# Main tiles of 128 positions of four batches, in five equal groups, in a load-heavy running-maximum kernel

## The chip, the cores and the metric

The kernel runs on one core of one Trainium2 chip. The metric is the device time of one execution in microseconds (us), median of several runs.

## The reference

```python
B, S, D = 8, 2048, 4096            # x is 268 MB of float32, w has 4096 elements
proj = (x @ w).squeeze(-1)         # one dot product per batch and position
cm = np.maximum.accumulate(proj, axis=1)
is_record = (proj >= cm).astype(np.float32)
return np.cumsum(is_record, axis=1)     # [8, 2048]
```

Every byte of `x` is used once. The scans afterwards are over 2048 values in each of 8 rows, so they are small.

## The kernel before

Positions 0 to 1919 are handled in four groups of 512, 512, 512 and 384 positions. A main tile is one batch of one group. Each of the 128 partitions gets `r` consecutive rows, `r` being 4 (a 64 KB run) or 3 (48 KB). Three buffers of 64 KB per partition take turns.

```python
for g in range(NG):                       # 4 groups, RS = (4, 4, 4, 3)
    r = RS[g]
    for t in range(B):                    # 8 tiles, one batch each
        i = SY.dma_start(
            out=at(g, t)[:, : r * D],
            in_=x[B - 1 - t, STARTS[g] : STARTS[g] + r * P, :].rearrange(
                "(p r) d -> p (r d)", r=r),
        ).then_inc(xs[t], 16)
        ...                               # waits until the tile three before is used up
```

Each row's dot product is divided by columns. VectorE multiplies and sums columns 0 to 2815 in one instruction. GpSimd multiplies columns 2816 to 4095 in place, and ScalarE then sums those products. At the end of a group, TensorE turns the partial sums into rows of 8 batches, and VectorE runs the scans.

```python
for j in range(r):
    i = dot(xb[:, j * D : j * D + VC], w_v[:, :VC], sum_v[...])      # VectorE
...
i = G.tensor_mul(out=xl, in0=xl, in1=w_sb).then_inc(pl, 1)           # GpSimd, one row
...
i = add_up(at(g, t)[:, j * D + VC : (j + 1) * D], sum_p[...])        # ScalarE
...
T.matmul(out=ps[:B, j : r * P : r], lhsT=l[...], rhs=identity, ...)  # 2 per row of the tile
```

The last 128 positions, the tail, come in tiles of 32 positions of four batches (2.1 MB, partitions ordered position first, then batch). The last two of these tiles are cut into smaller pieces. The change leaves this part alone, apart from the buffers it lands in.

## Time and profile before

| | before |
|---|---|
| time, median of 3 runs | 630.12 us |
| span in the profile | 629.3 us |
| busy: VectorE (DVE), GpSimd (POOL), ScalarE (ACT) | 65%, 59%, 29% |
| load queue, share of the 16 DMA engines' time | 98.9% |
| bytes read | 268.45 MB |

The first fence is from the page of the kernel before: busy time, the span in 40 slices (tenths busy), the load queue, and the chain of waits by engine.

```profile
PE 29.1 (5%) x96; PEld 13.5 (2%) x96; DVE 407.3 (65%) x294; ACT 181.2 (29%) x274; POOL 370.7 (59%) x149
...
DVE  0755775556766567755578655676556976655897
...
POOL 0554675456765557745577555676557666555775
...
DMA  9999999999999999999999999999999999999996
...
q1 hardware_dynamic: 6544, 268.50, 98.9%
...
DMA 16%; POOL 3%; DVE 2%; issue 1%; PE 1%; ACT 0%; SPq 0%
```

Only the DMA row has no gap. VectorE and GpSimd are five to seven tenths busy almost everywhere. The chain names only about a quarter of the span. It stops at 483 us, so its shares say little here.

The better reading comes from the moments at which loads land. GpSimd's first product of a tile waits for nothing but its load, so the timeline of GpSimd shows them. The columns are start, duration, line, operation and count, and in brackets the idle time just before and what ended it.

```profile
179.06 11.49 POOL L276 TENSOR_TENSOR xall<-xall,w_sb 128x1280 f32<-128x1280 f32 x4 [7.80 <-DMA xall<-in_x_dram]
198.36 11.50 POOL L276 TENSOR_TENSOR xall<-xall,w_sb 128x1280 f32<-128x1280 f32 x4 [7.81 <-DMA xall<-in_x_dram]
217.66 11.51 POOL L276 TENSOR_TENSOR xall<-xall,w_sb 128x1280 f32<-128x1280 f32 x4 [7.80 <-DMA xall<-in_x_dram]
...
512.45 8.64 POOL L276 TENSOR_TENSOR xall<-xall,w_sb 128x1280 f32<-128x1280 f32 x3 [5.86 <-DMA xall<-in_x_dram]
526.95 8.63 POOL L276 TENSOR_TENSOR xall<-xall,w_sb 128x1280 f32<-128x1280 f32 x3 [5.86 <-DMA xall<-in_x_dram]
...
609.34 2.90 POOL L336 TENSOR_TENSOR xall<-xall,w_sb 128x1280 f32<-128x1280 f32 x1 [0.39 <-DMA xall<-in_x_dram]
614.20 2.90 POOL L336 TENSOR_TENSOR xall<-xall,w_sb 128x1280 f32<-128x1280 f32 x1 [1.52 <-DMA xall<-in_x_dram]
```

Tiles of 8.39 MB come 19.30 us apart, tiles of 6.29 MB 14.50 us apart, and the tail's 2.10 MB tiles 4.86 us apart. These are 435, 434 and 432 GB/s. After each big tile GpSimd idles 7.8 us.

### The profile page before, as it was taken

The page shows a single profiled execution, that of the slowest core. Times are in us where ns is not written, and L with a number is a line of the kernel's source. Part 1 is how long each engine was busy: PE and PEld are TensorE (multiplying, and loading weights), DVE is VectorE, ACT ScalarE, POOL GpSimd, SP SyncE. Part 2 cuts the span into 40 slices and gives each one's busy share as a digit, 9 for nine tenths or more (in the row PEclk, how much of TensorE's full clock was granted, in tenths as well). Part 3 has the DMA queues.
Part 4 walks back from the last instruction along what each step waited for, and adds up shares of the span by engine and source line. Part 5 has one row for each costly group of instructions (what it writes and reads, how often), then busy time and mean ns, then how long its engine had stood idle before and what let it go on. Part 6 is the DMA issues. An engine that isn't in the chain of part 4 may idle for free. (4 is left out here: it accounts for less than half of the span.)

```text
span 629.3 us, 1140 instructions
## 1 busy us (share of the span) xinstructions
PE 29.1 (5%) x96; PEld 13.5 (2%) x96; DVE 407.3 (65%) x294; ACT 181.2 (29%) x274; POOL 370.7 (59%) x149
## 2 busy tenths in 40 slices
PE   8000000000020000000001000000002000000100
PEld 3000000000010000000000000000001000000000
DVE  0755775556766567755578655676556976655897
ACT  1222332223322233222233222332223232232254
POOL 0554675456765557745577555676557666555775
PEclk9999999999999999999996555555555555555565
DMA  9999999999999999999999999999999999999996
GB/s 401 400 467 400 446 421 425 442 437 429 442 425 450 417 450 417 459 408 458 408 458 408 458 408 458 408 459 408 462 418 438 416 447 441 413 447 444 404 425 248
DMA packets 6563, 268.54 MB, mean 427 GB/s; under 512 B 760, under 2 KB 1016, under 8 KB 1568
## 3 DMA queue, kind: packets, MB, share of 16 engines
q1 hardware_dynamic: 6544, 268.50, 98.9%
q10 hardware_dynamic: 16, 0.02, 0.0%
q14 instruction: 3, 0.02, 0.0%
HBM read 268.45 MB, written 0.07 MB: 427 GB/s over the span
## 5 line engine op out<-in xcount | busy, mean ns | idle before, releaser
L124 DVE CUSTOM_DVE_ANT_0 xall<-xall,w_v 128x2816 f32<-128x2816 f32 (+1 forms) x129 | 385.5, 3041 | 181.8 <-DMA xall<-in_x_dram 181.8
L276 POOL TENSOR_TENSOR xall<-xall,w_sb 128x1280 f32<-128x1280 f32 x120 | 345.0, 2909 | 246.7 <-DMA xall<-in_x_dram 243.3
L130 ACT ACTIVATE xall<-xall 128x1280 f32<-128x1280 f32 (+2 forms) x130 | 162.9, 1253 | 428.6 <-POOL xall L276 408.3
L312 PE MATMUL ps<-identity,small 128*8 128x128 f32 x60 | 13.0, 406 | 568.6 <-PEq L309 568.6
L130 ACT ACTIVATION_READ_ACCUMULATOR xall<-xall 128x1 f32 x130 | 24.2, 186 | 0.0
L336 POOL TENSOR_TENSOR xall<-xall,w_sb 128x1280 f32<-128x1280 f32 (+2 forms) x8 | 21.1, 2632 | 3.1 <-DMA xall<-in_x_dram 3.0
L312 PEld LDWEIGHTS ps<-identity,small 128*8 128x8 f32 x60 | 7.3, 125 | 575.4 <-issue 571.3
L140 DVE TENSOR_TENSOR_SCAN cm<-ps,cm,small 8x512 f32<-8x512 f32 (+3 forms) x8 | 7.0, 869 | 18.8 <-PE ps L312 18.4
L224 PE MATMUL w_v<-w,identity 8*128 8x512 f32 x14 | 12.1, 1056 | 0.0
L124 DVE DVE_READ_ACCUMULATOR2_ANT small<- 128x1 f32 x133 | 10.8, 81 | 0.0
L246 DVE MEMSET ps<- 8x512 f32 x1 | 0.5, 485 | 15.7 <-ACT w L235 15.7
L146 DVE TENSOR_TENSOR_SCAN cnt<-ps,cnt,small 8x512 f32<-8x512 f32 (+3 forms) x8 | 7.0, 870 | 0.3
L224 PEld LDWEIGHTS w_v<-w,identity 8*128 8x128 f32 x14 | 4.6, 332 | 7.3 <-issue 7.3
L143 DVE TENSOR_TENSOR ps<-ps,cm 8x512 f32<-8x512 f32 (+3 forms) x8 | 3.9, 487 | 0.3
L232 ACT COPY w_sb<-w_v 128x768 f32<-128x768 f32 x1 | 0.8, 799 | 11.4 <-PE w_v L224 11.4
L347 POOL TENSOR_TENSOR masked<-fold,small 128x4 f32<-128x4 f32 x8 | 1.6, 201 | 3.2 <-DVE small L124 3.2
L124 DVE CUSTOM_DVE_ANT_0 xall<-xall,w_v,small 128x480 f32<-128x480 f32 (+2 forms) x4 | 3.1, 810 | 0.2 <-DVE small L124 0.2
L357 PE MATMUL ps<-fold,masked 128*8 128x32 f32 x20 | 2.0, 235 | 25.3 <-ACT masked L352 17.7
L352 ACT ACTIVATE masked<-fold,small 128x4 f32<-128x4 f32 x10 | 3.0, 298 | 0.3
L336 POOL TENSOR_TENSOR xall<-xall,w 128x640 f32<-128x640 f32 (+1 forms) x2 | 2.3, 1137 | 0.1
L224 PE MATMUL ps<-w,identity 8*128 8x512 f32 x2 | 2.1, 1135 | 2.6 <-DMA w<-in_w_dram 2.6
L231 ACT ACT_TABLE_LOAD x1 | 1.3, 1283 | 2.7 <-DVE fold L242 2.7
(18 smaller groups left out, 5.3 us busy)
## 6 DMA issues: line engine op xcount, KB each, us to landing
xall<-in_x_dram SPq DMA_DIRECT2D x8, 6144.0 KB, 33.5
xall<-in_x_dram SPq DMA_DIRECT2D x6, 2048.0 KB, 42.4
xall<-in_x_dram SPq DMA_DIRECT2D x1, 1264.0 KB, 36.6
xall<-in_x_dram SPq DMA_DIRECT2D x1, 816.0 KB, 39.3
xall<-in_x_dram SPq DMA_DIRECT2D x1, 784.0 KB, 37.9
xall<-in_x_dram SPq DMA_DIRECT2D x2, 240.0 KB, 26.6
xall<-in_x_dram SPq DMA_DIRECT2D x1, 416.0 KB, 39.4
xall<-in_x_dram SPq DMA_DIRECT2D x24, 45.0
```

The source lines that it names most:

```text
L124: return V.tensor_tensor_reduce(out=xsl, in0=xsl, in1=wsl, scale=1.0, scalar=seed, op0=ALU.mult, op1=ALU.add, accum_out=dst,)
L130: return A.activation(out=xsl, in_=xsl, func=ACTF.Copy, accum_out=dst)
L140: V.tensor_tensor_scan(out=cm_, data0=src, data1=low, initial=cm0, op0=ALU.max, op1=ALU.max,)._wait_ge(psr, base).then_inc(psr, 1)
L143: V.tensor_tensor(out=src, in0=src, in1=cm_, op=ALU.is_ge)._wait_ge(psr, base + 1).then_inc(psr, 1)
L146: V.tensor_tensor_scan(out=cnt_, data0=src, data1=low, initial=cnt0, op0=ALU.add, op1=ALU.max,)._wait_ge(psr, base + 2).then_inc(cs, 1)
L224: i = T.matmul(out=dst, lhsT=identity[:NW, k : k + 1].to_broadcast([NW, P]), rhs=w_row, start=True, stop=True,).then_inc(bw, 1)
L276: i = G.tensor_mul(out=xl, in0=xl, in1=w_sb).then_inc(pl, 1)
L312: i = T.matmul(out=ps[:B, j : r * P : r], lhsT=l[:, j * B : (j + 1) * B], rhs=identity, start=k == 0, stop=k == 1,)
L336: G.tensor_mul(out=xl, in0=xl, in1=w_pool(*p))._wait_ge(xq[i], 16).then_inc(pl, 1)
L347: return eng.tensor_tensor(out=e, in0=by_b, in1=acc.to_broadcast([P, H]), op=ALU.mult)
L352: return A.activation(out=e, in_=by_b, func=ACTF.Copy, scale=acc)._wait_ge(pa, na).then_inc(ms, 1)
L357: return T.matmul(out=ps[:B, k * Q : (k + 1) * Q], lhsT=masked[:, n * B : (n + 1) * B], rhs=by_i, start=start, stop=stop,)
```

## The change

Its intent is one loop with equal tiles. The main part becomes five groups of 384 positions, each of six tiles. A tile holds 128 positions of four batches, and each partition still gets one 64 KB run (four consecutive rows of one batch). The differently sized last group disappears, and so does the code that existed only for it. GpSimd multiplies four rows in one instruction. Since a tile now mixes four batches over the partitions, GpSimd adds and masks the sums before TensorE turns them. The last main tile is loaded in two halves, so that work on it can start earlier. The diff, cut to its core:

```diff
-    RS = (4, 4, 4, 3)
-    R = RS[0]
+    R = 4
+    NC = 3
+    NT = NC * B // H          # 6 tiles a group
+    N = NC * P                # 384 positions a group
+    NG = 5
...
-            for t in range(B):
-                    in_=x[B - 1 - t, STARTS[g] : STARTS[g] + r * P, :].rearrange(
-                        "(p r) d -> p (r d)", r=r
+            for t in range(NT):
+                b0, s0 = t % 2 * H, STARTS[g] + t // 2 * P
+                src = x[b0 : b0 + H, s0 : s0 + P, :].rearrange(
+                    "b (q r) d -> q b (r d)", r=R
+                )
+                if last and g == NG - 1:          # two halves
+                    i = SY.dma_start(out=at(t)[:, :half], in_=src[:, :, :half]).then_inc(xs[t], 16)
+                    SY.dma_start(out=at(t)[:, half:], in_=src[:, :, half:]).then_inc(xh, 16)
+                else:
+                    i = SY.dma_start(out=at(t), in_=src).then_inc(xs[t], 16)
...
-                    i = G.tensor_mul(out=xl, in0=xl, in1=w_sb).then_inc(pl, 1)
+                n = R // 2 if t == NT - 1 else R
+                for j in range(0, R, n):
+                    xl = rows[:, j : j + n, VC:]
+                    i = G.tensor_mul(out=xl, in0=xl, in1=w_one.to_broadcast([P, n, PC])).then_inc(pl, 1)
+            G.tensor_tensor(out=sum_t, in0=sum_v, in1=sum_p, op=ALU.add)...
+            G.tensor_tensor(out=gmask..., in0=sum_t..., in1=by_b..., op=ALU.mult)...
...
-            for j in range(r):
-                for k, l in enumerate((sum_p, sum_v)):
-                        out=ps[:B, j : r * P : r], lhsT=l[:, j * B : (j + 1) * B],
-                        rhs=identity, start=k == 0, stop=k == 1,
+            for j in range(R):
+                for c in range(NC):
+                        out=ps[:B, c * P + j : (c + 1) * P : R],
+                        lhsT=gmask[:, k * B : (k + 1) * B],
+                        rhs=by_i, start=True, stop=True,
```

More of the change, by code (lines that the diff above doesn't have):

```diff
@@ L41 @@
     NW = D // WC
-    RS = (4, 4, 4, 3)
-    R = RS[0]
+    R = 4
     NS = 3
-    NG = len(RS)
-    NL = NG - 1
-    N = R * P
-    STARTS = [sum(RS[:g]) * P for g in range(NG)]
-    S0 = sum(RS) * P
-    assert S0 + P == S
+    H = 4
+    Q = P // H
+    NC = 3
+    NT = NC * B // H
+    N = NC * P
+    NG = 5
+    STARTS = [g * N for g in range(NG)]
+    S0 = NG * N
+    assert S0 + P == S and NT % NS == 0
     VC = 2816
@@ L53 @@
     CV = 3584
-    H = 4
-    Q = P // H
     LAST = [
@@ L87 @@
     w_sb = sb([P, PC], "w_sb")
-    cm = sb([B, N], "cm")
-    cnt = sb([B, N], "cnt")
+    cm = sb([B, N + P], "cm")
+    cnt = sb([B, N + P], "cnt")
+    gmask = sb([P, R * NC * B], "gmask")
     masked = sb([P, 10 * B], "masked")
@@ L102, in cut @@
         return small[:, off[0] - n : off[0]]
-    sum_v, sum_p = cut(R * B), cut(R * B)
+    sum_v, sum_p, sum_t = (cut(R * NT) for _ in range(3))
     acc_v, acc_p = cut(B - 2), cut(B - 2)
@@ L112, in sem @@
         return tc.alloc_semaphore(f"{name}_{next(ns)}")
-    xs = [sem("xs") for _ in range(B)]
-    fr = [sem("fr") for _ in range(B)]
+    xs = [sem("xs") for _ in range(NT)]
+    fr = [sem("fr") for _ in range(NT)]
     xq = [sem("xq") for _ in TILES]
-    ws, bw, wc, cs, od, oe, psr, pd, pl, go, sd, pa, con, fo, ms, p7, mg, pg, ml = (
-        sem(n) for n in "ws bw wc cs od oe psr pd pl go sd pa con fo ms p7 mg pg ml".split()
+    ws, bw, wc, cs, od, oe, psr, pd, pl, xh, sd, pa, con, fo, ms, p7, mg, pg, ml, mk = (
+        sem(n) for n in "ws bw wc cs od oe psr pd pl xh sd pa con fo ms p7 mg pg ml mk".split()
     )
@@ L148, in scans, with at, col_of @@
         )._wait_ge(psr, base + 2).then_inc(cs, 1)
-    def at(g, t):
-        return xbuf[(t if g < NL else t + NS - 1) % NS]
+    def at(t):
+        return xbuf[t % NS]
     def user_before(g, t):
-        if t >= NS:
-            return t - NS, g + 1
-        if g == NL:
-            return B - NS + t, g
-        return max(u for u in range(B) if u % NS == t), g
+        return (t - NS, g + 1) if t >= NS else (t + NT - NS, g)
     def free(u, n):
-        return (p7, n) if u == B - 1 else (fr[u], 2 * n)
+        return (p7, n) if u == NT - 1 else (fr[u], 2 * n)
+    def col_of(t, j):
+        return (j * NC + t // 2) * 2 + t % 2
     with tc.tile_critical(no_gpsimd_drain=True):
         for g in range(NG):
-            r = RS[g]
-            for t in range(B):
-                i = SY.dma_start(
-                    out=at(g, t)[:, : r * D],
-                    in_=x[B - 1 - t, STARTS[g] : STARTS[g] + r * P, :].rearrange(
-                        "(p r) d -> p (r d)", r=r
-                    ),
-                ).then_inc(xs[t], 16)
-                u, n = user_before(g, t)
+            for t in range(NT):
[3 more added lines that the diff above has]
+                )
+                half = R // 2 * D
+                last = t == NT - 1
+                u, n = user_before(g, t)
+                if last and g == NG - 1:
+                    i = SY.dma_start(
+                        out=at(t)[:, :half], in_=src[:, :, :half]
+                    ).then_inc(xs[t], 16)
+                    SY.dma_start(
+                        out=at(t)[:, half:], in_=src[:, :, half:]
+                    ).then_inc(xh, 16)
+                else:
+                    i = SY.dma_start(out=at(t), in_=src).then_inc(xs[t], 16)
+                    if last:
+                        SY.sem_inc(xh, 16)
                 if n:
-                    i._wait_ge(*(free(u, n)))
+                    i._wait_ge(*free(u, n))
                 if g == t == 0:
@@ L182 @@
                     SY.dma_start(
-                        out=out[:, STARTS[g - 1] : STARTS[g]], in_=cnt
+                        out=out[:, STARTS[g - 1] : STARTS[g]], in_=cnt[:, :N]
                     )._wait_ge(cs, g + 1).then_inc(od, 16)
         def slot(m):
-            if m < NS:
-                return None, xbuf[m][:, RS[-1] * D :]
-            u = B - NS if m < 2 * NS else B - NS + 1
-            return u, at(NL, u)[:, (m % NS) * D : (m % NS + 1) * D]
-        freed = {None}
+            u = NT - NS + m // 4
+            return u, at(u)[:, m % 4 * D : (m % 4 + 1) * D]
+        freed = set()
         for i, (m, c0, c1, _, _) in enumerate(TILES):
@@ L215 @@
         G.memset(masked, 0.0).then_inc(con, 1)
-        G.memset(cm[:, N - 1 :], NEG).then_inc(con, 1)
-        G.memset(cnt[:, N - 1 :], 0.0).then_inc(con, 1)
+        G.memset(cm[:, N - 1 : N], NEG).then_inc(con, 1)
+        G.memset(cnt[:, N - 1 : N], 0.0).then_inc(con, 1)
         T.wait_ge(con, 2)
@@ L246 @@
         V.memset(ps[:B, :N], LOW)._wait_ge(wc, 3).then_inc(psr, 1)
-        def group_scans(r=R):
-            n = r * P
-            scans(cm[:, :n], cnt[:, :n], ps[:B, :n], cm[:, N - 1 :], cnt[:, N - 1 :])
-        def group_dots(r, g=0):
-            for t in range(B):
-                b, xb = B - 1 - t, at(g, t)
-                for j in range(r):
-                    i = dot(
-                        xb[:, j * D : j * D + VC], w_v[:, :VC],
-                        sum_v[:, j * B + b : j * B + b + 1],
-                    )
-                    if j == 0:
-                        i._wait_ge(xs[t], 16)
-                i.then_inc(fr[t], 1)
@@ L264, with group_scans, landed @@
-        with V.Fori(0, NL):
+        def group_scans():
+            scans(
+                cm[:, :N], cnt[:, :N], ps[:B, :N], cm[:, N - 1 : N], cnt[:, N - 1 : N]
+            )
+        def landed(i, t, j):
+            if j == 0:
+                i._wait_ge(xs[t], 16)
+            elif t == NT - 1 and j == R // 2:
+                i._wait_ge(xh, 16)
+        with V.Fori(0, NG):
             group_scans()
             V.sem_inc(psr, -3)
-            group_dots(R)
-        group_scans()
-        V.sem_inc(psr, -3)
@@ L270 @@
-        group_dots(RS[-1], NL)
-        def group_products(r, g=0):
-            for t in range(B):
-                for j in range(r):
-                    xl = at(g, t)[:, j * D + VC : (j + 1) * D]
-                    i = G.tensor_mul(out=xl, in0=xl, in1=w_sb).then_inc(pl, 1)
-                    if j == 0:
-                        i._wait_ge(xs[t], 16)
-        G.wait_ge(wc, 3)
-        with G.Fori(0, NL):
-            group_products(R)
-            G.wait_ge(pg, 1).then_inc(pg, -1)
-        group_products(RS[-1], NL)
@@ L286, in group_sums @@
-        def group_sums(r, g=0):
-            for t in range(B):
-                b = B - 1 - t
-                for j in range(r):
-                    i = add_up(
-                        at(g, t)[:, j * D + VC : (j + 1) * D],
-                        sum_p[:, j * B + b : j * B + b + 1],
-                    )._wait_ge(pl, j + 1)
+            for t in range(NT):
+                xb = at(t)
+                for j in range(R):
+                    c = col_of(t, j)
+                    i = dot(
+                        xb[:, j * D : j * D + VC], w_v[:, :VC], sum_v[:, c : c + 1]
+                    )
+                    landed(i, t, j)
+                i.then_inc(fr[t], 1)
@@ new lines @@
+        G.wait_ge(wc, 3)
+        w_one = w_sb.rearrange("p (o c) -> p o c", o=1)
+        with G.Fori(0, NG):
+            for t in range(NT):
+                rows = at(t).rearrange("p (r d) -> p r d", r=R)
+                n = R // 2 if t == NT - 1 else R
+                for j in range(0, R, n):
+                    xl = rows[:, j : j + n, VC:]
+                    i = G.tensor_mul(
+                        out=xl, in0=xl, in1=w_one.to_broadcast([P, n, PC])
+                    ).then_inc(pl, 1)
+                    landed(i, t, j)
+            G.tensor_tensor(
+                out=sum_t, in0=sum_v, in1=sum_p, op=ALU.add
+            )._wait_ge(fr[NT - 1], 2).then_inc(mk, 1)
+            G.tensor_tensor(
+                out=gmask.rearrange("p (k b) -> p k b", b=H),
+                in0=sum_t.rearrange("p (k o) -> p k o", o=1).to_broadcast(
+                    [P, R * NT, H]
+                ),
+                in1=by_b.rearrange("p (o b) -> p o b", o=1).to_broadcast(
+                    [P, R * NT, H]
+                ),
+                op=ALU.mult,
+            )._wait_ge(mk, 1).then_inc(mk, 1)
+            G.wait_ge(pg, 1).then_inc(pg, -1)
@@ L294, in group_sums @@
+        with A.Fori(0, NG):
+            for t in range(NT):
+                for j in range(R):
+                    c = col_of(t, j)
+                    i = add_up(
+                        at(t)[:, j * D + VC : (j + 1) * D], sum_p[:, c : c + 1]
+                    )
+                    if j == 0 or t == NT - 1 and j == R // 2:
+                        i._wait_ge(pl, 1)
+                    if j == R - 1 or t == NT - 1 and j == R // 2 - 1:
+                        A.sem_inc(pl, -1)
                 i.then_inc(fr[t], 1)
-                A.sem_inc(pl, -r)
@@ L296, in group_sums @@
             A.wait_ge(pd, 1).then_inc(pd, -1)
-        with A.Fori(0, NL):
-            group_sums(R)
-        group_sums(RS[-1], NL)
-        def group_rows(r):
-            T.wait_ge(fr[B - 1], 2).then_inc(p7, 1)
-            T.sem_inc(fr[B - 1], -2)
-            if r == R:
-                for s in xs:
-                    T.sem_inc(s, -16)
-                T.sem_inc(pg, 1)
+        with T.Fori(0, NG):
+            T.wait_ge(mk, 2).then_inc(p7, 1)
+            T.sem_inc(mk, -2)
+            T.sem_inc(fr[NT - 1], -2)
+            for s in (*xs, xh):
+                T.sem_inc(s, -16)
+            T.sem_inc(pg, 1)
@@ L309, in group_rows @@
             T.wait_ge(od, 16).then_inc(od, -16)
-            for j in range(r):
-                for k, l in enumerate((sum_p, sum_v)):
+            for j in range(R):
+                for c in range(NC):
+                    k = j * NC + c
                     i = T.matmul(
-                        out=ps[:B, j : r * P : r], lhsT=l[:, j * B : (j + 1) * B],
-                        rhs=identity, start=k == 0, stop=k == 1,
-                    )
-                    if j == r - 1:
-                        i.then_inc((pd, psr)[k], 1)
@@ L319 @@
-        with T.Fori(0, NL):
-            group_rows(R)
-        group_rows(RS[-1])
+                        out=ps[:B, c * P + j : (c + 1) * P : R],
+                        lhsT=gmask[:, k * B : (k + 1) * B],
+                        rhs=by_i, start=True, stop=True,
+                    )
+                    if k == 0:
+                        i.then_inc(pd, 1)
+            i.then_inc(psr, 1)
         nv = npool = na = 0
@@ L376 @@
             if m == 2:
-                group_scans(RS[-1])
+                group_scans()
             if m == 4:
```

## The prediction

Its 630.4 us is the measured time before (630.1 us) plus an estimate of 0.3 us for tiles of four pieces. The 434.6 GB/s in it is the rate in the trace of before.

> **What bounds the kernel.** The loads. The slices view shows the DMA at 9 tenths in every slice but the last; the queue table gives one load queue 98.9%. VectorE is busy 65% of the span, GpSimd 59%, ScalarE 29%. In GpSimd's timeline the first product of each 8.39 MB tile (which waits only for its load) starts every 19.30 us in the middle of the run (179.06, 198.36, 217.66, 236.96): 434.6 GB/s. The 6.29 MB tiles of the last group come every 14.5 us (512.45, 526.95, 541.44): 434 GB/s. The tail's 2.10 MB tiles, already in the 4-batch layout, land 4.85 us apart (609.30, 614.15): 432 GB/s. [...] At 434.6 GB/s the 268.45 MB alone take 618 of the 629.3 us. The rest is start-up, about 2 us lost in the first six tiles (spacings up to 20.0 us), about 2 us of sums after the last bytes, and 2.9 us for storing the result.
>
> **What the change does to that.** It moves the same bytes: 24 x 19.30 + 8 x 14.50 = 579 us of main tiles become 30 x 19.30 = 579 us. Each partition still receives one contiguous 64 KB run; the tile is now four 2 MB pieces, 32 MB apart, instead of one 8 MB piece. The tail's tiles and the final store are unchanged.
>
> **What it adds off the critical path.** GpSimd's product becomes one instruction of 4 rows (11.5 us, four at 2.9), so ScalarE's four sums (1.45 us each) start later: a buffer comes free about 17.4 us after landing rather than 13. Its next load has to be issued within 38.6 us of the landing (two tiles are queued), so the DMA doesn't notice. Each group gains two mask operations on GpSimd (at 2.3 ns an element 1.1 us, estimated, perhaps 2); the transposes shrink from 16 matmuls over 128 columns (3.2 us) to 12 over 32 (about 1.5), the scans from 3.2 to 2.6 us. VectorE starts a group 1 to 2 us after its tile has landed, with 7 us of slack per tile. At the end the halved last tile leaves VectorE 2 rows of backlog (6.1 us) instead of 3 (9.1 us). GpSimd and VectorE catch up by the fifth tail tile, as VectorE does now (idle 0.62 us before 609.30). On the critical path: nothing gained, nothing lost.
>
> **Prediction.** 630.4 us, range 628.5 to 633.5; faster by over 2%: 0.01; within 2%: 0.94; slower by over 2%: 0.05. The 0.3 us is for tiles of four pieces; if all lost the tail's 0.5%, it would be 633.
>
> **What would show it.** Right: tiles landing every 19.3 us through all five groups, DMA at 9 tenths in all slices, last tail load landing near 624 us, GpSimd's products near 11.5 us with 7 us idle per tile, the chain of waits led by loads. Wrong: tile spacing above 19.4 us; a load that waits for its buffer until the queue is empty; VectorE or GpSimd not idle before the fifth tail tile.
>
> **What would make it wrong.** Reading at large power-of-two distances: [...]the tail's loads with the same step don't show it. Second: the broadcast operand could slow the 4-row product beyond 19.3 us.

## The result, and the profile after

| | before | after |
|---|---|---|
| median | 630.24 us (4 runs) | 631.12 us (4 runs) |
| fastest to slowest | 630.04 to 630.52 | 630.69 to 631.40 |
| ratio | | 1.0013, 95% interval 0.9996 to 1.0030 |
| span in the profile | 629.3 us | 629.3 us |

The two kernels are the same within 2%, and both results are correct. A ratio here is the mean time of one kernel's fast runs over that of the other's in the same rounds, so it is not quite the ratio of the medians. The page of the kernel after, the same parts as shown of before:

```profile
PE 23.2 (4%) x156; PEld 12.7 (2%) x156; DVE 407.0 (65%) x297; ACT 171.7 (27%) x274; POOL 360.8 (57%) x74
...
DVE  0655775567765557865567666677556875559887
...
POOL 0444675455764447754467654576445675449585
...
DMA  9999999999999999999999999999999999999995
...
q1 hardware_dynamic: 6416, 268.50, 98.8%
...
DMA 72%; POOL 18%; ACT 7%; issue 2%; SPq 0%; DVE 0%; PE 0%
```

The load queue moved the same 268.50 MB and is as full as before. GpSimd executes 74 instructions instead of 149 and saves 9.9 us, ScalarE saves 9.5 us and TensorE 5.9 us. None of it shows in the time.

The chain of waits now puts 18% on GpSimd and 7% on ScalarE. It walks from a load to the release of that load's buffer, and so passes through the product and the sums of every third tile. That the chain goes through a release doesn't make it the limit: two more loads stood in the queue at the time (a main tile landed 41.7 us after its issue in the median, over two spacings of 19.3 us). The experiment with little compute tests this below.

The timeline of GpSimd, after:

```profile
178.33 11.05 POOL L288 TENSOR_TENSOR xall<-xall,w_sb 128x5120 f32<-128x5120 f32 x1 [8.26 <-DMA xall<-in_x_dram]
197.62 11.05 POOL L288 TENSOR_TENSOR xall<-xall,w_sb 128x5120 f32<-128x5120 f32 x1 [8.24 <-DMA xall<-in_x_dram]
216.92 11.05 POOL L288 TENSOR_TENSOR xall<-xall,w_sb 128x5120 f32<-128x5120 f32 x1 [8.25 <-DMA xall<-in_x_dram]
236.28 11.20 POOL L288 TENSOR_TENSOR xall<-xall,w_sb 128x2560 f32<-128x2560 f32 x2 [8.32 <-DMA xall<-in_x_dram]
250.21 0.23 POOL L292 TENSOR_TENSOR small<-small 128x24 f32<-128x24 f32 x1 [2.73 <-ACT xall L131]
250.52 0.34 POOL L295 TENSOR_TENSOR gmask<-small,fold 128x96 f32<-128x96 f32 x1
255.59 11.05 POOL L288 TENSOR_TENSOR xall<-xall,w_sb 128x5120 f32<-128x5120 f32 x1 [4.72 <-DMA xall<-in_x_dram]
...
609.43 2.90 POOL L354 TENSOR_TENSOR xall<-xall,w_sb 128x1280 f32<-128x1280 f32 x1 [0.83 <-DMA xall<-in_x_dram]
614.27 2.90 POOL L354 TENSOR_TENSOR xall<-xall,w_sb 128x1280 f32<-128x1280 f32 x1 [1.51 <-DMA xall<-in_x_dram]
```

Tiles again come 19.29 to 19.36 us apart, also over the edge of a group (236.28 to 255.59, 19.31 us). Even there GpSimd, with its two new instructions done, waits 4.7 us for the load. The two tail tiles shown land within 0.1 us of where they landed before.

### The profile page after: what moved, and what is told of

Same layout as the page of the kernel before. It is cut to its first block, busy times and chain, and to the rows that moved or that the text cites. A ratio compares the mean times of both kernels' runs of the same rounds, so it can differ in the third digit from the quotient of the medians.

```text
span 629.3 us, 1240 instructions
## 1 busy us (share of the span) xinstructions
PE 23.2 (4%) x156; PEld 12.7 (2%) x156; DVE 407.0 (65%) x297; ACT 171.7 (27%) x274; POOL 360.8 (57%) x74
## 3 DMA queue, kind: packets, MB, share of 16 engines
q1 hardware_dynamic: 6416, 268.50, 98.8%
HBM read 268.45 MB, written 0.07 MB: 427 GB/s over the span
## 4 chain that ended last, share of the span: by engine, by line
DMA 72%; POOL 18%; ACT 7%; issue 2%; SPq 0%; DVE 0%; PE 0%
DMA xall<-in_x_dram 72%; POOL xall L288 18%; ACT xall L131 7%; SPq L204 0%; POOL xall L354 0%; PE ps L375 0%; SPq L182 0%; ACT masked L370 0%; DVE cm L141 0%; DVE cnt L147 0%; DVE ps L144 0%; SPq L460 0%; SPq L163 0%
## 5 line engine op out<-in xcount | busy, mean ns | idle before, releaser
L288 POOL TENSOR_TENSOR xall<-xall,w_sb 128x5120 f32<-128x5120 f32 (+1 forms) x35 | 332.2, 9499 | 242.1 <-DMA xall<-in_x_dram 242.1
L332 PE MATMUL ps<-fold,gmask 128*8 128x32 f32 x120 | 7.2, 240 | 572.7 <-PEq L328 572.7
L141 DVE TENSOR_TENSOR_SCAN cm<-ps,cm,small 8x384 f32<-8x384 f32 (+2 forms) x9 | 6.9, 765 | 23.6 <-PE ps L332 23.2
L332 PEld LDWEIGHTS ps<-fold,gmask 128*8 128x8 f32 x120 | 6.5, 114 | 574.8 <-issue 574.8
L147 DVE TENSOR_TENSOR_SCAN cnt<-ps,cnt,small 8x384 f32<-8x384 f32 (+2 forms) x9 | 6.9, 767 | 0.3
L144 DVE TENSOR_TENSOR ps<-ps,cm 8x384 f32<-8x384 f32 (+2 forms) x9 | 3.9, 435 | 0.3
L375 PE MATMUL ps<-fold,masked 128*8 128x32 f32 x20 | 2.0, 234 | 27.1 <-ACT masked L370 18.1
## 6 DMA issues: line engine op xcount, KB each, us to landing
xall<-in_x_dram SPq DMA_DIRECT2D x29, 41.7
```

The source lines that it names most:

```text
L141: V.tensor_tensor_scan(out=cm_, data0=src, data1=low, initial=cm0, op0=ALU.max, op1=ALU.max,)._wait_ge(psr, base).then_inc(psr, 1)
L144: V.tensor_tensor(out=src, in0=src, in1=cm_, op=ALU.is_ge)._wait_ge(psr, base + 1).then_inc(psr, 1)
L147: V.tensor_tensor_scan(out=cnt_, data0=src, data1=low, initial=cnt0, op0=ALU.add, op1=ALU.max,)._wait_ge(psr, base + 2).then_inc(cs, 1)
L288: i = G.tensor_mul(out=xl, in0=xl, in1=w_one.to_broadcast([P, n, PC])).then_inc(pl, 1)
L332: i = T.matmul(out=ps[:B, c * P + j : (c + 1) * P : R], lhsT=gmask[:, k * B : (k + 1) * B], rhs=by_i, start=True, stop=True,)
L375: return T.matmul(out=ps[:B, k * Q : (k + 1) * Q], lhsT=masked[:, n * B : (n + 1) * B], rhs=by_i, start=start, stop=stop,)
```

## The experiments

The theory was that the load queue alone sets the time: both kernels move the same bytes at the same rate, and everything else hides beneath. There were two rivals. One says that effects cancel: tiles of four distant pieces cost some microseconds, and leaner groups gain them back. The other says that the engines are close to limiting. All kernels but the repeat of the kernel before are variants of the kernel after.

### The kernel after again

No edit; it is the base for the variants that ran in the same rounds.

> The kernel after, unchanged, as a base for its variants on the same chip and to see whether its median, 0.9 us above the kernel before, is real. Theory (the load queue alone sets the time, both kernels move the same bytes at the same rate): ratio to the kernel before within 1.000 to 1.002. Rival (two effects of some us cancel): same here, so this run is only the base.

Measured: 631.01 us (5 runs, 630.75 to 631.04) against 630.23 us for before (9 runs, 630.07 to 630.47), ratio 1.0010, interval 0.9997 to 1.0024. The medians differ by 0.8 us, as they did in the first comparison by 0.9 us. The interval still includes 1, yet in neither comparison was any run of after as fast as the slowest of before (the execution profiled first, 631.05 us, was not among them), so a small difference is likely.

### One contiguous piece per tile

```diff
# cut: the two half loads of the last tile index src to match
-                src = x[b0 : b0 + H, s0 : s0 + P, :].rearrange("b (q r) d -> q b (r d)", r=R)
+                n0 = (g * NT + t) * R * P
+                src = x.rearrange("b s d -> (b s) d")[n0 : n0 + R * P].rearrange(
+                    "(p r) d -> p (r d)", r=R)
```

> The kernel after with each main tile read as one contiguous 8.39 MB piece (512 consecutive rows) instead of four 2 MB pieces 32 MB apart; everything else is kept, so the result is wrong on purpose. Theory: the four pieces cost nothing, so within 0.7 us of the kernel after, tiles still 19.3 us apart. Rival: the four pieces cost time and leaner groups gain it back, then this run has the gain alone and is at least 2 us faster than both kernels.

Measured: 630.74 us (5 runs, 630.43 to 631.17), 0.3 us below the kernel after. The two ranges overlap, so the times alone do not separate these kernels. The rival of cancelling effects needed at least 2 us and falls. The traces place what small cost there is. Here are the first GpSimd products in this run, and then in the kernel after.

```profile
22.96 11.05 POOL L288 TENSOR_TENSOR xall<-xall,w_sb 128x5120 f32<-128x5120 f32 x1 [20.96 <-DMA xall<-in_x_dram]
42.25 11.05 POOL L288 TENSOR_TENSOR xall<-xall,w_sb 128x5120 f32<-128x5120 f32 x1 [8.24 <-DMA xall<-in_x_dram]
```

```profile
23.66 11.05 POOL L288 TENSOR_TENSOR xall<-xall,w_sb 128x5120 f32<-128x5120 f32 x1 [21.67 <-DMA xall<-in_x_dram]
42.97 11.05 POOL L288 TENSOR_TENSOR xall<-xall,w_sb 128x5120 f32<-128x5120 f32 x1 [8.25 <-DMA xall<-in_x_dram]
```

The very first tile lands 0.7 us later with four pieces, and the second keeps that distance. The first product starts at 23.4 to 23.7 us in the traces of the kernel after, its repeat, and the two-more, one-load and little-compute runs below. It starts at 22.9 to 23.0 us in the four traces with contiguous tiles (this run, the four-streams run and both traces of before). Between the repeat of after and the repeat of before, the final store's issue moves by the same amount: 626.13 against 625.49 us. In this run, which differs from the kernel after in the walk alone, it is at 625.50 us. So the traces put a one-time cost of about 0.6 us on the first load, and no cost on later tiles. Why the first load is slower was not tested.

### Little compute

```diff
-  dot(xb[:, j * D : j * D + VC], w_v[:, :VC], sum_v[:, c : c + 1])
+  dot(xb[:, j * D : j * D + 512], w_v[:, :512], sum_v[:, c : c + 1])
   # and GpSimd's products and ScalarE's sums: 256 columns a row instead of 1280
```

> The kernel after with the main tiles' dots cut to 512 of 2816 columns and products and sums to 256 of 1280 (wrong result on purpose); loads unchanged. Theory: compute is wholly hidden, so within 0.7 us of the kernel after although VectorE and GpSimd lose four fifths of their main work. Rival (the engines or their contention with the loads hold the kernel back): at least 3 us faster.

Measured: 631.04 us (5 runs), 0.03 us from the kernel after. Its page:

```profile
PE 23.2 (4%) x156; PEld 12.7 (2%) x156; DVE 119.6 (19%) x297; ACT 69.3 (11%) x274; POOL 100.2 (16%) x74
...
DVE  0310111120111103111011221011111111101487
...
POOL 0110111110111101111001111011110111101465
...
DMA  9999999999999999999999999999999999999995
```

VectorE fell from 407 to 120 us of work and GpSimd from 361 to 100 us, and the time stayed. This is the plainest evidence that the GpSimd and ScalarE shares in the chain of waits above are not a limit, and that none of the 25 us of engine time saved by the change could have shown.

### Two and four more reductions per tile

```diff
                     landed(i, t, j)
+                for e in range(2 if t < NT - 1 else 0):        # 4 in the second run
+                    i = V.tensor_reduce(out=spare[...], in_=w_v[:, :VC], op=ALU.add, ...)
                 i.then_inc(fr[t], 1)
```

> The kernel after with two more VectorE reductions of 2816 columns (about 3 us each) after the dots of every main tile but a group's last: VectorE's work per such tile about 18.1 us against a load every 19.3 us. The result stays right. Theory: still hidden, 630 to 633 us. Rival (VectorE is close to limiting): about 30 x 6 us more at worst, anything above 640 us speaks for it.

> The same with four more reductions: about 24 us of VectorE per tile against 19.3 us of load. Theory: now VectorE is the limit; per group 5 x 24.1 + 12.1 + about 6.6 for masks, transposes and scans = 139 us, five groups from 23.7 us on, then the tail's dots: about 750 us, range 740 to 765. If instead the time grows from the two-more run by the added work in proportion, there was no slack.

Measured: 630.82 us with two more (4 runs) and 746.47 us with four more (2 runs), both with correct results. Two more raised VectorE's busy time from 407.0 to 556.7 us, 89% of the span, at no cost. From that run's page:

```profile
PE 23.2 (4%) x156; PEld 12.7 (2%) x156; DVE 556.7 (89%) x347; ACT 171.7 (27%) x274; POOL 360.5 (57%) x74
...
DMA  9999999999999999999999999999999999999996
```

With four more it is the limit (704.2 us busy, 95% of a span of 744.3 us). The waits of the DMA queue itself, in the kernel after and then in the run with four more (who was waited for, us in total, times, longest):

```profile
SPq L182 <- ACT xall L131: 435.3, 22, 37.0
```

```profile
SPq L183 <- DVE small L280: 559.1, 22, 44.8
```

In the kernel after, the issue of a load waits mostly for ScalarE's last sum. With four more it waits for VectorE's extra reductions. The waiting alone says nothing, as the issuing engine waits for hundreds of microseconds in both. What counts is whether the DMA engines run dry meanwhile, and the slices of the run with four more show that they do:

```profile
DMA  9999999899988898987997797977898988797770
```

In the kernel after this row has a 9 in every slice but the last. The estimate of 750 us from 24.1 us per tile was 0.5% too high.

### Fewer bytes

```diff
-                    i = SY.dma_start(out=at(t), in_=src).then_inc(xs[t], 16)
+                    cut_ = R * D if g == 0 else R * D * 7 // 8
+                    i = SY.dma_start(out=at(t)[:, :cut_], in_=src[:, :, :cut_]).then_inc(xs[t], 16)
```

> The kernel after with 23 main tiles (all of groups 2 to 5 but the last) loading 7 of 8 parts of each 64 KB run; compute unchanged, so the last half row is stale and the result wrong on purpose. Theory: the time falls one for one with the bytes, 23 x 19.31 / 8 = 55.5 us, to about 575 us (572 to 579). Rival (compute or group handling nearly limits): clearly less than 55 us saved.

Measured: 575.53 us (4 runs), 55.3 us less than the run with two more reductions of the same rounds and 55.6 us less than the first four runs of after. The prediction from bytes alone was 55.5 us. GpSimd's timeline of this run:

```profile
171.02 11.04 POOL L291 TENSOR_TENSOR xall<-xall,w_sb 128x5120 f32<-128x5120 f32 x1 [5.86 <-DMA xall<-in_x_dram]
187.89 11.03 POOL L291 TENSOR_TENSOR xall<-xall,w_sb 128x5120 f32<-128x5120 f32 x1 [5.83 <-DMA xall<-in_x_dram]
```

The spacing is 16.87 us, 7/8 of 19.30 (16.89). Time follows bytes one for one, with the engines' work unchanged.

### The last main tile in one load

The two halves of the last tile are the one part of the change that touches the end of the run, so it was undone alone.

```diff
-                if last and g == NG - 1:
-                    ...two loads...
-                else:
-                    i = SY.dma_start(out=at(t), in_=src).then_inc(xs[t], 16)
-                    if last:
-                        SY.sem_inc(xh, 16)
+                i = SY.dma_start(out=at(t), in_=src).then_inc(xs[t], 16)
+                if last:
+                    SY.sem_inc(xh, 16)
```

> The kernel after with its last main tile in one load instead of two (result stays right). Worked out from the trace of after: GpSimd then starts the tail's products at about 600.7 us instead of 595.2, 2.9 us of product and some overhead each against a load every 4.85 us, so it is still about 1.5 us behind at the last small pieces: 1 to 2 us slower than the kernel after. Rival (nothing at the end matters because all is load-bound): no change, within 0.4 us.

Measured: 632.87 us (5 runs, 632.59 to 632.90), 1.9 us above the kernel after of the same rounds; ratio to before 1.0041, interval 1.0027 to 1.0054. The expected 1 to 2 us came, and GpSimd's first tail product started at 600.51 us (worked out: 600.7). Here it is in the kernel after, and then in this run:

```profile
595.15 2.91 POOL L354 TENSOR_TENSOR xall<-xall,w_sb 128x1280 f32<-128x1280 f32 x1 [1.91 <-POOLq L305]
```

```profile
600.51 2.90 POOL L346 TENSOR_TENSOR xall<-xall,w_sb 128x1280 f32<-128x1280 f32 x1 [1.95 <-POOLq L297]
```

So the halves do earn about 1.9 us. They repair a delay that the new tiles bring with them: without them GpSimd enters the tail 5.4 us later (600.51 instead of 595.15) and is still behind when the last bytes land. A smaller delay is absorbed: in the run with two more reductions this product started at 597.92 us, and the time stayed at 630.82 us. Work was hidden here only as long as more loads followed.

### The kernel before again

> The kernel before, unchanged, for a second trace. In the first trace four of its first six tiles landed 0.2 to 0.7 us late (1.8 us in all). If that belongs to the kernel (loads of new batches, or its instruction fetches) it comes again; if it was a disturbance from outside, tiles land 19.3 us apart from the start, and the last load lands earlier, near 622.5 us. Time 630.2 us, ratio 1.000.

Measured: 630.23 us (5 runs), ratio 1.000. First products in the second trace of before:

```profile
42.17 11.50 POOL L276 TENSOR_TENSOR xall<-xall,w_sb 128x1280 f32<-128x1280 f32 x4 [7.78 <-DMA xall<-in_x_dram]
61.50 11.50 POOL L276 TENSOR_TENSOR xall<-xall,w_sb 128x1280 f32<-128x1280 f32 x4 [7.83 <-DMA xall<-in_x_dram]
80.88 11.49 POOL L276 TENSOR_TENSOR xall<-xall,w_sb 128x1280 f32<-128x1280 f32 x4 [7.88 <-DMA xall<-in_x_dram]
100.19 11.50 POOL L276 TENSOR_TENSOR xall<-xall,w_sb 128x1280 f32<-128x1280 f32 x4 [7.82 <-DMA xall<-in_x_dram]
120.26 5.76 POOL L276 TENSOR_TENSOR xall<-xall,w_sb 128x1280 f32<-128x1280 f32 x2 [8.57 <-DMA xall<-in_x_dram]
```

In the first trace these products started at 42.12, 62.06, 81.69, 101.19 and 121.17 us. Three of its four late tiles (1.1 us together) do not come again, so they were a disturbance of that one execution. The fourth does (100.19 to 120.26, 20.07 us). In both traces the DMA records show two 8 KB packets of kind "instruction" in that tile, each beside a lengthened 64 KB packet (in the first trace 0.31 us each, at 105 and 117 us, beside 64 KB packets of 2.96 and 2.66 us instead of 2.42). The kernel after has such packets at 131 us and 589 us, and by the landing records the loads they fell into came about 0.2 and 1.0 us late. That these packets cause the delay is an inference from their position. The final store was issued at 625.49 us in this trace and at 626.39 us in the first, so the equal spans of the two first profiles (629.3 us) were partly luck.

### The source walked in another order

The remaining runs ask how far the layout could have gone wrong: the prediction had named large power-of-two distances as its main risk. All give wrong results on purpose, and each is one look.

```diff
-  src = x[b0 : b0 + H, s0 : s0 + P, :].rearrange("b (q r) d -> q b (r d)", r=R)   # 32 x 4 x 64 KB
+  # batch by batch, 4 x 32 x 64 KB:
+  src = x[b0 : b0 + H, s0 : s0 + P, :].rearrange("b (q r) d -> b q (r d)", r=R)
+  # four streams on one contiguous piece, written as 4 x 32 x 64 KB:
+  src = flat[n0 : n0 + R * P].rearrange("(e q r) d -> e q (r d)", e=4, r=R)
+  # 16 places, 2 MB apart, 16 x 8 x 64 KB:
+  src = x[m0 % B].rearrange("(e s) d -> e s d", e=16)[:, k : k + 32].rearrange("e (q r) d -> e q (r d)", r=R)
+  # the same, 2 MB + 16 KB apart:
+  src = flat[o : o + 16 * 129].rearrange("(e s) d -> e s d", e=16)[:, :32].rearrange("e (q r) d -> e q (r d)", r=R)
```

> The kernel after with the main tiles' source walked batch by batch (4 x 32 x 64 KB) instead of position by position (32 x 4 x 64 KB); the same bytes and run lengths, partitions in another order, so the result is wrong on purpose. If [...] only 4 of 16 engines work: a tile takes about 77 us and the run about 2,360 us. Rival (only run length and bytes count): 631 us.

Measured: 2688.53 us. The slices of this run:

```profile
DMA  2222222222222222222222222222222222222473
GB/s 55 59 61 62 66 66 68 71 76 81 88 98 107 109 109 108 106 109 109 109 109 105 109 109 109 109 106 108 109 109 109 108 106 109 109 109 109 137 179 116
```

The DMA is at 2 tenths (0.25 in the windows view), so the work of four of 16 engines is done, as expected. In the steady part a 64 KB packet takes 2.42 us, which is 27.1 GB/s, and four times that is the 109 GB/s of the slices. The change's own walk, 32 x 4, fills all 16 (98.8% on the page of after). The first third was not expected: 55 to 98 GB/s until about 800 us, then the 109 GB/s of four full engines.

> The kernel after with each main tile read from 16 places 2 MB apart in one batch (16 x 8 x 64 KB[...]); wrong result on purpose. If streams that run in step a large power of two apart disturb each other (the four engines of the batch-by-batch run, 32 MB apart, needed 4.8 us a packet at first and 2.42 later), packets take longer than 2.42 us at least at first: 650 to 830 us. Rival (that was something else): 631 us, all packets 2.42 us.

> Four engines as in the batch-by-batch run, but on one contiguous 8.39 MB piece (4 x 32 x 64 KB, the four streams 2 MB apart instead of 32 MB). If the distance of 32 MB made that run's first third slow: 109 GB/s from the start, tiles 77.4 us apart, about 2,365 us. Rival (four engines are slow at first whatever the distance, a matter of time or of start-up): again about 2,690 us.

> As the run with 16 places 2 MB apart, but the places are 2 MB + 16 KB apart (129 rows of 16 KB instead of 128); same bytes, run lengths, loop order and engines, wrong result on purpose. Theory (the power of two is what hurts): packets back near 2.42 us, 629 to 640 us. Rival (any 16 places far apart are slow, or the walk itself is): again near 1,263 us.

Measured: 1263.05 us (16 places 2 MB apart), 630.32 us (four streams on one piece), 1261.95 us (2 MB + 16 KB apart). The slices of the first and of the last of these three:

```profile
DMA  9999999999999999999999999999999999999998
GB/s 200 208 222 202 200 206 220 206 200 206 216 210 200 200 223 210 200 200 214 218 200 200 214 218 200 200 212 220 200 200 212 216 204 200 206 222 204 199 295 339
```

```profile
DMA  9999999999999999999999999999999999999998
GB/s 200 212 221 200 200 206 223 204 200 200 225 208 200 200 225 208 200 200 223 210 200 200 210 223 200 200 204 227 202 200 200 229 204 200 200 225 208 198 298 337
```

All 16 engines are busy the whole time, yet move half: a 64 KB packet takes 5.1 us in the DMA records instead of 2.42 (16 engines at 64 KB in 5.1 us make 206 GB/s, as the rows show). The padded run rules my theory out as it was stated. Taking 2 MB + 16 KB instead of 2 MB changed nothing, so an exact power of two is not needed. Its rival, that any 16 places far apart or this walk itself are slow, stands and was not split further. The run with four streams was inconclusive: it took 630.32 us, so its 268.45 MB came at 426 GB/s on average, and at 27.1 GB/s each that takes nearly all 16 engines. Its source is one contiguous piece, and nothing here shows in what order the chip read it.

What halves the rate stays open. The packet records of the batch-by-batch run, joined into four chains by their times, show how its slow part ended. The first eight packets of each chain took 3.9 to 5.3 us. Soon one in every four got shorter, then two, then three: in one chain the durations repeat as 4.9, 4.9, 4.9, 3.0 us at 100 us, as 5.0, 5.0, 2.7, 2.5 us at 400 us and as 2.4, 2.4, 4.5, 2.7 us at 700 us, and after 850 us all but seven of the 64 KB packets take 2.42 us. Four 64 KB packets are 256 KB of source. What the period comes from, and why one run recovers and the 16-place runs do not, no run tested.

## Why the prediction was right

- **"The loads" bound the kernel: right, and shown.** Removing an eighth of 23 tiles' bytes took away 55 us, four fifths less VectorE dot work in the main tiles took away nothing, and over a third more VectorE work (407 to 557 us) added nothing.
- **"24 x 19.30 + 8 x 14.50 = 579 us of main tiles become 30 x 19.30 = 579 us": right.** Tiles landed 19.3 us apart through all five groups, including group edges.
- **Work added off the critical path: right in kind, with sizes a little off.** GpSimd's product of four rows took 11.05 us (predicted 11.5). A buffer came free 16.2 us after its load had landed (42.97 to 59.20 in the trace of after; predicted 17.4). The two mask operations took 0.57 us (estimated 1.1, which at 2.3 ns an element, from the 2.909 us of a 1280-column product before, is some 480 elements a partition, where the two have 24 and 96 columns). The transposes took 1.4 us (about 1.5).
- **The end: right.** VectorE was idle 1.06 us before the fifth tail tile, at 609.38 us. The halves matter here: in one load, the last tile costs 1.9 us.
- **"The 0.3 us is for tiles of four pieces": the size is near, the place was wrong.** The medians differ by 0.8 to 0.9 us, with intervals that include a ratio of 1. The traces show no cost per tile but about 0.6 us once, at the first load.
- **"About 2 us lost in the first six tiles":** about 1.1 us of it belonged to one execution and not to the kernel. It did no harm, as the total had been taken from the measured time.
- **The stated risk:** the tile spacings show no cost of distance in the change; whether the 0.6 us at the first load come from it was not tested. The evidence that carried the prediction was that the tail's loads already used the same walk at 432 GB/s. Its reasoning about distance did not reach what really can go wrong, which the 16-place runs show: a walk of 16 x 8 distant runs in place of 32 x 4 halved the rate (1263.05 us against 631), for a reason that is still open.

## What to carry to other kernels

Where one queue is full from start to end, count its bytes and find its rate. Here changes that altered neither moved only the ends of the run: four fifths less dot work left the time at 631.04 us (631.01 beside it), and one load in place of two at the end cost 1.9 us. Judge a chain of waits that runs through buffer releases by whether a release comes later than the loads already queued, and shrink the work to be sure. When the walk of a load changes, look for a load in the same kernel that already walks that way: with runs of 64 KB throughout, other walks made the run two to over four times as long here (1263.05 and 2688.53 us against 631).
